# One strided tensor_reduce in place of three adds, in a kernel that subtracts the mean of every four rows

## The chip, the cores and the metric

One core of a Trainium2 chip. The metric is the device time of one execution in microseconds (us). Every time compared below is of runs in the fast state; the granted clock was 1.0 throughout. The two probe runs (p1, p2) ran once each, state unknown; only durations of single instructions are read from them. VectorE, the engine that does the sums, is called DVE in the profile. Data are worked on in SBUF, in 128 partitions (the 128 of the shapes in the profile); 16 DMA engines (the profile gives the queues' shares of 16) move them in (loads) and out (stores).

## The reference

```python
x_r = x.reshape(B, S // 4, 4, D)            # x: (8, 4096, 2112), float32
pooled = x_r.mean(axis=2)
return x - np.repeat(pooled, 4, axis=1)     # each row minus the mean of its group of four
```

## The kernel before

A group of four rows lies in one SBUF partition, 4 x 2112 = 8448 numbers one behind the other. 128 groups make a tile, and there are 64 tiles. For each: a load, three adds that make the sum `s`, one broadcast multiply-and-add that subtracts a quarter of it in place, and a store.

```python
STRIDE = 4
IO_BUFS = 6
# ... cut ...
    io_pool = ctx.enter_context(tc.tile_pool(name="io", bufs=IO_BUFS))
    sum_pool = ctx.enter_context(tc.tile_pool(name="sum", bufs=1))

    for g0 in range(0, G, P):
        gsz = min(P, G - g0)
        x_tile = io_pool.tile([P, W], mybir.dt.float32)
        nc.sync.dma_start(out=x_tile[:gsz], in_=xg[g0:g0 + gsz])

        rows = x_tile[:gsz].rearrange("p (f d) -> p f d", f=STRIDE)
        s = sum_pool.tile([P, D], mybir.dt.float32)
        nc.vector.tensor_add(out=s[:gsz], in0=rows[:, 0, :], in1=rows[:, 1, :])
        for f in range(2, STRIDE):
            nc.vector.tensor_add(out=s[:gsz], in0=s[:gsz], in1=rows[:, f, :])
        nc.vector.scalar_tensor_tensor(
            out=rows,
            in0=s[:gsz, None, :].to_broadcast([gsz, STRIDE, D]),
            scalar=-1.0 / STRIDE,
            in1=rows,
            op0=mybir.AluOpType.mult,
            op1=mybir.AluOpType.add,
        )
        nc.scalar.dma_start(out=og[g0:g0 + gsz], in_=x_tile[:gsz])
```

## Time and profile before

| | before |
|---|---|
| time, median | 1286.5 us |
| span in the profile | 1284.7 us |
| mean transfer rate over the span | 431 GB/s |
| VectorE busy | 1026.1 us (80%) |
| VectorE per tile: three adds, one subtract | 7.07 + 8.96 us |
| period of a tile in the middle | 19.95 us |

The rate is the row to start with: the 16 DMA engines are busy in practically every slice (the two queues take 50.0 and 49.9% of their time), so the kernel is bound by its transfers. The last three rows give the room that VectorE has in a tile; the prediction works it out and shows the lines behind the table.

### The profile page before, as it was taken

The page shows a single profiled execution, that of the slowest core. Times are in us where ns is not written, and L with a number is a line of the kernel's source. Part 1 is how long each engine was busy: PE and PEld are TensorE (multiplying, and loading weights), DVE is VectorE, ACT ScalarE, POOL GpSimd, SP SyncE. Part 2 cuts the span into 40 slices and gives each one's busy share as a digit, 9 for nine tenths or more (in the row PEclk, how much of TensorE's full clock was granted, in tenths as well). Part 3 has the DMA queues.
Part 4 walks back from the last instruction along what each step waited for, and adds up shares of the span by engine and source line. Part 5 has one row for each costly group of instructions (what it writes and reads, how often), then busy time and mean ns, then how long its engine had stood idle before and what let it go on. Part 6 is the DMA issues. An engine that isn't in the chain of part 4 may idle for free.

```text
span 1284.7 us, 674 instructions
## 1 busy us (share of the span) xinstructions
DVE 1026.1 (80%) x256; POOL 0.2 (0%) x4
## 2 busy tenths in 40 slices
DVE  5998778787787877878778787787887878778784
POOL 0000000000000000000000000000000000000000
DMA  9999999999999999999999999999999999999998
GB/s 404 421 438 438 433 425 437 438 427 432 437 437 426 435 437 431 429 437 437 431 428 438 437 431 429 437 436 432 428 438 436 430 430 437 437 426 433 438 431 380
DMA packets 18437, 553.70 MB, mean 431 GB/s; under 512 B 2048, under 2 KB 2048, under 8 KB 2048
## 3 DMA queue, kind: packets, MB, share of 16 engines
q1 hardware_dynamic: 9216, 276.83, 50.0%
q10 hardware_dynamic: 9216, 276.83, 49.9%
q14 instruction: 5, 0.04, 0.0%
HBM read 276.82 MB, written 276.82 MB: 431 GB/s over the span
## 4 chain that ended last, share of the span: by engine, by line
DVE 80%; another core or an unknown queue 17%; DMA 1%; issue 1%; DVEq 0%
DVE x_tile L46 45%; DVE s L45 24%; DVE s L43 12%; DMA x_tile<-in_x_dram 1%; DVEq L43 0%
## 5 line engine op out<-in xcount | busy, mean ns | idle before, releaser
L46 DVE SCALAR_TENSOR_TENSOR x_tile<-s,x_tile 128x8448 f32<-128x8448 f32 x64 | 573.3, 8958 | 2.2
L43 DVE TENSOR_TENSOR s<-x_tile 128x2112 f32<-128x2112 f32 x64 | 150.9, 2358 | 237.5 <-DMA x_tile<-in_x_dram 237.3
L45 DVE TENSOR_TENSOR s<-s,x_tile 128x2112 f32<-128x2112 f32 x128 | 301.8, 2358 | 4.4
L69 POOL MEMSET const-bfloat16-1.0<- 128x1 bf16 x1 | 0.1, 103 | 0.0
L69 POOL MEMSET const-uint8-127<- 128x1 uint8 x1 | 0.1, 102 | 0.0
L69 POOL MEMSET const-float32-0.0<- 128x1 f32 x1 | 0.1, 100 | 0.2 <-issue 0.2
L69 POOL MEMSET const-float32-1.0<- 128x1 f32 x1 | 0.1, 99 | 0.0
## 6 DMA issues: line engine op xcount, KB each, us to landing
x_tile<-in_x_dram SPq DMA_DIRECT2D x64, 4224.0 KB, 59.6
out_dram<-x_tile ACTq DMA_DIRECT2D x64, 4224.0 KB, 43.8
```

Of the source, the lines that this page charges most:

```text
L43: nc.vector.tensor_add(out=s[:gsz], in0=rows[:, 0, :], in1=rows[:, 1, :])
L45: nc.vector.tensor_add(out=s[:gsz], in0=s[:gsz], in1=rows[:, f, :])
L46: nc.vector.scalar_tensor_tensor(out=rows, in0=s[:gsz, None, :].to_broadcast([gsz, STRIDE, D]), scalar=-1.0 / STRIDE, in1=rows, op0=mybir. ...
L69: nc = _bacc.Bacc("TRN2", target_bir_lowering=False, num_devices=1)
```

## The change

Its intent: one instruction for the sum instead of three, with fewer fixed costs and no partial sums written and read back.

```diff
-        nc.vector.tensor_add(out=s[:gsz], in0=rows[:, 0, :], in1=rows[:, 1, :])
-        for f in range(2, STRIDE):
-            nc.vector.tensor_add(out=s[:gsz], in0=s[:gsz], in1=rows[:, f, :])
+        nc.vector.tensor_reduce(
+            out=s[:gsz],
+            in_=rows.rearrange("p f d -> p d f"),
+            op=mybir.AluOpType.add,
+            axis=mybir.AxisListType.X,
+        )
```

## The prediction

"The full rate" is that of line 46: 8958 ns for 8448 elements and 2358 for the adds' 2112 are 1.04 ns per element and 158 ns of fixed cost, and the 0.16 and 158 below are this cost. The forecast's sum came to 1286.5 + about 1.5 = 1288. The first rival's came to 1552.

> **What bounds the kernel now.** I read the page from the top: busy shares, then DMA in slices, then the queues, to see which resource has no slack; then the groups of instructions, for what one VectorE (DVE) tile costs; then two stretches of the trace, to see who waits for whom in the middle and what the end hangs on.
>
> ```profile
> span 1284.7 us, 674 instructions
> DVE 1026.1 (80%) x256; POOL 0.2 (0%) x4
> ...
> DMA  9999999999999999999999999999999999999998
> ...
> q1 hardware_dynamic: 9216, 276.83, 50.0%
> q10 hardware_dynamic: 9216, 276.83, 49.9%
> ...
> HBM read 276.82 MB, written 276.82 MB: 431 GB/s over the span
> ```
>
> The 16 DMA engines are at 90% or more in every slice but the last; one queue loads, the other stores, and together they take 99.9% of the engines' time. The bytes are already the least possible (x read once, the result written once). VectorE is busy 80% only. So the bound is DMA; VectorE counts only if it becomes slower than a tile's transfers. How far is that?
>
> ```profile
> L46 DVE SCALAR_TENSOR_TENSOR x_tile<-s,x_tile 128x8448 f32<-128x8448 f32 x64 | 573.3, 8958 | 2.2
> L43 DVE TENSOR_TENSOR s<-x_tile 128x2112 f32<-128x2112 f32 x64 | 150.9, 2358 | 237.5 <-DMA x_tile<-in_x_dram 237.3
> L45 DVE TENSOR_TENSOR s<-s,x_tile 128x2112 f32<-128x2112 f32 x128 | 301.8, 2358 | 4.4
> ```
>
> There are 64 tiles. Each has one add at line 43, two at line 45 (3 x 2.358 = 7.074 us) and one broadcast subtract at line 46 (8.958 us): 16.03 us busy. Nearly all of VectorE's idle time, 237.3 us, stands before the first add of a tile and is a wait for the load of x.
>
> ```profile
> 1194.25 2.36 DVE L43 TENSOR_TENSOR s<-x_tile 128x2112 f32<-128x2112 f32 x1 [3.83 <-DMA x_tile<-in_x_dram]
> ...
> 1214.20 2.36 DVE L43 TENSOR_TENSOR s<-x_tile 128x2112 f32<-128x2112 f32 x1 [3.81 <-DMA x_tile<-in_x_dram]
> ```
>
> A tile starts every 1214.20 - 1194.25 = 19.95 us, and VectorE sits idle 3.8 us of it. Between instructions lie about 0.03 us: early tiles, whose data lie ready, follow each other at 29.23 - 13.05 = 16.18 us, 0.14 more than the busy sum, for four instructions. So 3.8 us per tile is the room that the change may use up. The end, in five stretches:
>
> ```profile
> 1234.00:1254.00 20.00, 16.04 (x4) 0.00 (x0) 1.00 1.01 434
> 1254.00:1262.00 8.00, 7.78 (x4) 0.00 (x0) 1.00 0.95 410
> 1262.00:1270.00 8.00, 8.00 (x1) 0.00 (x0) 1.00 1.03 444
> 1270.00:1278.00 8.00, 0.26 (x1) 0.00 (x0) 1.00 1.01 435
> 1278.00:1285.00 7.00, 0.00 (x0) 0.00 (x0) 1.00 0.39 169
> ```
>
> The last load has landed at 1254, the last subtract ends at 1270.26 and the last store follows. From 1270 on 8 x 435 + 7 x 169 = 4.66 thousand KB move, where one store is 4.33 (4224 KB): when the last store is issued, only 0.33 MB of earlier stores is left, 0.8 us at 435 GB/s. In this tail VectorE is on the path almost in full.
>
> [...]
>
> **The change part by part.** Removed: 3 x 64 adds, 452.7 us of VectorE. Added: 64 reduces that read x_tile as (d, f), so successive reads lie 2112 x 4 = 8448 bytes apart and every fourth returns to the next column. Instruction order shows nothing else moves: loads and stores keep order and queues, the six x buffers and the single s stay, so there are still two dependent groups per tile, on one engine. Gaps fall from four to two, 0.07 us less.
>
> Cost at the full rate[...], as line 46 has it. That is 1.88 us more than the three adds, not less[...]. A tile takes 8.96 + 8.96 + 0.07 = 17.99 us. This is below 19.95, so it lies beside the transfers and the wait of 3.8 us shrinks to about 1.95. Buffers: a tile's load takes 59.6 us to land, its work 16, its store 43.8, and 119.4 is six periods of 19.95 (119.7): the loop is full because the DMA queues are, so 1.9 us more on VectorE just leaves 1.9 us less queueing. The start too: by the third store at 31 + 2 x 18 = 67 us there is work for at least 10 transfers of 10 us, so DMA never runs dry. The end: 1.88 us later less the 0.8 us of backlog used up, so +1.1 to +1.9. Sum: 1286.5 + about 1.5 = 1288.
>
> **The rivals.** First, VectorE becomes the bound because of the stride. The room is a reduce of 19.95 - 8.96 - 0.07 = 10.92 us, or (10.92 - 0.16)/8.448 = 1.27 ns per element. [...] with the first load (13.05 us before the first add), 13.7 for the last store without backlog, and 1.8 for the difference between timed run and span: 1552. At half rate (2.08 ns) 17.76 us and 1743[...]. For it: each successive element hops[...]. [...]
>
> Second, the gain that the change seems to intend: three instructions into one, fewer fixed costs. Two saved of 158 ns each are 20 us over 64 tiles, but VectorE isn't the bound[...]. Even an impossibly short reduce would save only part of the 16 us in the tail, at most 7 us or 0.5%. Faster by over 2% has no path.
>
> Third, the reduce at full rate, but 18 us too near to 19.95, so that jitter in loads starves the queues. The waits in the middle are even (3.71 to 3.85 us), and up to three tiles queue ahead; I give it next to nothing, 1290 to 1295 at most.
>
> **Range and chances.** Two outcomes, nothing much between: full rate and 1288, or a stride penalty. I lean to the full rate, 58 in 100[...]; I put 28 on penalties up to about 1.75 ns per element (1300 to 1560) and 13 on worse. The time is the first mode, put at 1289 to lean slightly to the rivals. The range must reach from the first mode through the second: 1284 to 1570, about 86%, the remainder above. Slower by 2% means 1312, a reduce beyond about 11 us, so nearly any penalty above 1.29 ns.
>
> **What would show it.** Right: one line of 64 TENSOR_REDUCE with a mean near 8957 ns, VectorE busy 64 x 17.92 = 1147 us (89%), the wait for loads cut from 237 to about 120 us, DMA still at 9 in every slice, the span longer by 1 to 2 us. Wrong: a reduce mean above 10.9 us; then the wait for loads vanishes after the first tile, VectorE stands near 98%, and the DMA digits fall to 8 or 7. If the reduce is slow but the time unchanged, the room was misread; if it is near 9 us and the time over 1295, the queue argument failed.

## The result, and the profile after

The changed kernel takes 1529.8 us (median of 5 runs, 1529.76 to 1530.04), the kernel before 1286.5 on the same chip. The ratio is 1.189, 95% interval 1.187 to 1.191: slower. Here and below, a ratio is the mean time of one kernel's fast runs over that of the other's of the same rounds, so it isn't quite the ratio of the medians quoted.

First the changed kernel's page: busy shares, the span in 40 slices (a digit is a busy share in tenths), the bytes moved.

```profile
span 1528.3 us, 546 instructions
...
DVE 1498.2 (98%) x128; POOL 0.2 (0%) x4
...
DVE  6999999999999999999999999999999999999996
...
DMA  9999899989899998998998989998989899889535
...
HBM read 276.82 MB, written 276.82 MB: 362 GB/s over the span
```

VectorE has gone from 80% to 98% and is busy 90% or more in every slice but the first and the last. The DMA digits, 9 in all slices but one before, drop to 8 in many slices and near the end to 3: the engines now wait for work. The same bytes move at 362 instead of 431 GB/s. The bound has changed hands. The groups of instructions of the changed kernel say which one did it, and its landing times what became of the queues:

```profile
L44 DVE TENSOR_REDUCE s<-x_tile 128x2112 f32<-128x8448 f32 x64 | 924.9, 14452 | 15.6 <-DMA x_tile<-in_x_dram 13.4
L50 DVE SCALAR_TENSOR_TENSOR x_tile<-s,x_tile 128x8448 f32<-128x8448 f32 x64 | 573.3, 8958 | 2.2
...
x_tile<-in_x_dram SPq DMA_DIRECT2D x64, 4224.0 KB, 21.2
out_dram<-x_tile ACTq DMA_DIRECT2D x64, 4224.0 KB, 22.6
```

The subtract is unchanged at 8958 ns. The reduce takes 14452 ns where the three adds took 3 x 2358 = 7074. The adds (2112 elements, 2358 ns) and the subtract (8448, 8958) lie on a line of 1.04 ns per element and 158 ns of fixed cost. Less that 158, the reduce takes 14294 / 8448 = 1.69 ns per element read. The wait for loads, 237.3 us before, is 13.4, the one before the first tile. A load now lands in 21.2 us (59.6 before) and a store in 22.6 (43.8): the queues are short, and a buffer spends its time with VectorE (an estimate from these medians: with six buffers, one comes round in six periods of 23.48, 140.9 us; its transfers take 43.8 of it, where they took 103.4 of 119.7 before). One tile in the timeline of the changed kernel:

```profile
1234.31 14.45 DVE L44 TENSOR_REDUCE s<-x_tile 128x2112 f32<-128x8448 f32 x1
...
1248.80 8.96 DVE L50 SCALAR_TENSOR_TENSOR x_tile<-s,x_tile 128x8448 f32<-128x8448 f32 x1
1257.79 14.45 DVE L44 TENSOR_REDUCE s<-x_tile 128x2112 f32<-128x8448 f32 x1
```

The period is 1257.79 - 1234.31 = 23.48 us, and the span adds up: 13.4 before the first reduce, 64 x 23.48 = 1502.7, and 12.3 from the end of the last subtract (1516.0) to the end, together 1528.4. The end of the changed kernel in three stretches (VectorE busy, then DMA share and GB/s last):

```profile
1504.00:1512.00 8.00, 7.97 (x2) 0.00 (x0) 1.00 0.00 0
1512.00:1520.00 8.00, 4.02 (x1) 0.00 (x0) 1.00 0.47 203
1520.00:1529.00 9.00, 0.00 (x0) 0.00 (x0) 1.00 0.70 300
```

While VectorE finishes the last tile, nothing moves at all; the last store then starts on idle engines.

### The profile page after: what moved, and what is told of

Same layout as the page of the kernel before. It is cut to its first block, busy times and chain, and to the rows that moved or that the text cites. A ratio compares the mean times of both kernels' runs of the same rounds, so it can differ in the third digit from the quotient of the medians.

```text
span 1528.3 us, 546 instructions
## 1 busy us (share of the span) xinstructions
DVE 1498.2 (98%) x128; POOL 0.2 (0%) x4
## 2 busy tenths in 40 slices
DMA packets 18436, 553.69 MB, mean 362 GB/s; under 512 B 2048, under 2 KB 2048, under 8 KB 2048
## 4 chain that ended last, share of the span: by engine, by line
DVE 98%; DMA 1%; issue 0%
DVE s L44 61%; DVE x_tile L50 38%; DMA x_tile<-in_x_dram 1%
## 5 line engine op out<-in xcount | busy, mean ns | idle before, releaser
L44 DVE TENSOR_REDUCE s<-x_tile 128x2112 f32<-128x8448 f32 x64 | 924.9, 14452 | 15.6 <-DMA x_tile<-in_x_dram 13.4
L50 DVE SCALAR_TENSOR_TENSOR x_tile<-s,x_tile 128x8448 f32<-128x8448 f32 x64 | 573.3, 8958 | 2.2
## 6 DMA issues: line engine op xcount, KB each, us to landing
x_tile<-in_x_dram SPq DMA_DIRECT2D x64, 4224.0 KB, 21.2
out_dram<-x_tile ACTq DMA_DIRECT2D x64, 4224.0 KB, 22.6
```

The costliest lines, as they stand in the source:

```text
L44: nc.vector.tensor_reduce(out=s[:gsz], in_=rows.rearrange("p f d -> p d f"), op=mybir.AluOpType.add, axis=mybir.AxisListType.X,)
L50: nc.vector.scalar_tensor_tensor(out=rows, in0=s[:gsz, None, :].to_broadcast([gsz, STRIDE, D]), scalar=-1.0 / STRIDE, in1=rows, op0=mybir. ...
```

## The experiments

Three questions. Is it the stride, or the reduce as such, that makes 14.45 us? Does the length of VectorE's tile explain the time? And what would a reduce at the full rate have given? The diffs are shortened; `...` stands for what is left out.

**e1_adjacent: the same reduce over neighbours.** The result is wrong (each group of four is four columns of one row).

```diff
-            in_=rows.rearrange("p f d -> p d f"),
+            in_=x_tile[:gsz].rearrange("p (d f) -> p d f", f=STRIDE),
```

> Same reduce of groups of four, but over four neighbouring elements instead of over the four rows (the result is wrong on purpose). Theory 1 (the stride is what costs): the reduce takes about 8.96 us,[...] VectorE is busy 89%, and the time is 1288 us, as the first branch of the prediction had it. Theory 2 (a reduce in groups of four is slow whatever it reads): 14.45 us and about 1530 us as in the changed kernel. If the reduce takes 9 us and the time is still over 1295, my reading of the room beside the transfers is wrong.

(The subtract over as many elements took 8958 ns in the kernel before.)

Measured: 1318.6 us, ratio 1.025 (1.024 to 1.027). From this run's page:

```profile
L44 DVE TENSOR_REDUCE s<-x_tile 128x2112 f32<-128x8448 f32 x64 | 573.0, 8953 | 154.5 <-DMA x_tile<-in_x_dram 154.2
...
HBM read 276.82 MB, written 276.82 MB: 420 GB/s over the span
```

The same instruction, the same shapes, the same number of groups: 8953 ns instead of 14452. So the addresses cost the 5.5 us, and the reduce as such does not. But the time is not the 1288 that went with that branch, though VectorE waits 154 us for loads, so it isn't the bound. The transfers themselves are slower, 420 in place of 431 GB/s. That part of my reading was wrong; e6 to e8 go after it.

**p1_patterns: what a hop costs.** The changed kernel with four x buffers, and on the first four tiles 18 extra instructions into a scratch tile, each on its own line. For instance:

```diff
+            nc.vector.tensor_reduce(out=scr[:, 0:W // 2].rearrange("p (b d) -> p b d", d=4224),
+                in_=x_tile[:, 0:W].rearrange("p (b f d) -> p b d f", f=2, d=4224), op=..., axis=...)
```

> The changed kernel with four x buffers; the first four tiles also run 18 probe instructions into a scratch tile, each on a line of its own (time of the whole is of no interest; results stay right). Theory 1[...]: groups of four at hop 1 take 8.96 us; every other hop (2, 4, 16, 24, 64, 1056, 2112 words) is slower, 14 us or more[...]; pairs of neighbours and then a hop take 8.96. Theory 2: all groups of four take 14.45, groups of two 19.9 (5.49 us too much for 2112 groups is 2.6 ns a group), groups of eight 11.7. Theory 3 (a single read stream is free to alternate between two regions, and it is four regions or the distance that costs): groups of two at 4096 and 4224 words take 8.53 and 8.96 us, while groups of four and eight are slow; hop 2048 instead of 2112 tells whether the distance matters. A copy that reads the same hops, and an add with one hopping source, say whether other instructions pay as well[...].

The result was right; the run took 2350.9 us, which means nothing here. "Group" is how many elements are summed, "hop" the distance in 4-byte words from one to the next. Eight of its groups of instructions:

```profile
L49 DVE TENSOR_REDUCE scr<-x_tile 128x2112 f32<-128x8448 f32 x4 | 60.4, 15109 | 0.1
L64 DVE TENSOR_TENSOR scr<-x_tile 128x8448 f32<-128x8448 f32 x4 | 59.0, 14754 | 0.1
...
L54 DVE TENSOR_REDUCE scr<-x_tile 128x2112 f32<-128x8448 f32 x4 | 57.8, 14453 | 0.1
...
L57 DVE TENSOR_REDUCE scr<-x_tile 128x4224 f32<-128x8448 f32 x4 | 36.2, 9041 | 0.1
...
L63 DVE TENSOR_TENSOR scr<-x_tile 128x8448 f32<-128x8448 f32 x4 | 35.8, 8958 | 0.1
L60 DVE TENSOR_REDUCE scr<-x_tile 128x1056 f32<-128x8448 f32 x4 | 35.8, 8953 | 0.1
...
L48 DVE TENSOR_REDUCE scr<-x_tile 128x2112 f32<-128x8448 f32 x4 | 35.8, 8944 | 0.0
...
L62 DVE COPY scr<-x_tile 128x8448 f32<-128x8448 f32 x4 | 29.7, 7415 | 0.1
```

L54 is the reduce of the change. L49 is a group of four at a hop of only 4 words: as slow, even slower. Hops of 16, 24, 64 and 1056 words lie between 14274 and 14523, and 2048 words (8 KiB) at 14017 for its 8192 elements, the same rate (1.69 ns per element). So the distance hardly matters. L57 is a group of **two**, 4224 words apart: 9041, nearly free; at 4096 words (16 KiB) 8773 for 8192 elements. Groups of eight at 1056 words: 14341. L60 reads two neighbours before each hop: free (8953). A hop of 1 is free (8948), and L48, a hop of 2 words, is free too, against theory 1. L64 is an add one of whose sources goes over the four rows: 14754 against 8958 for the contiguous add in L63, and the copy pays as well (L62, 7415 against 4559 contiguous). Theory 2 falls. Theory 3 fits the large hops: two regions in turn are free, four are not.

**p2_patterns: where the edge lies.** Fourteen more probes built the same way.

> A second set of 14 probes on the first four tiles (time of the whole of no interest). In the first set groups of four over four regions took 14.45 us at hops of 64, 1056 and 2112 words, over two regions 9.04, groups of four at hop 2 words 8.94, pairs of neighbours then a hop 8.95. Theory P[...]: groups of two are free at any hop (about 9.0 us at 2, 4, 16, 24); groups of three at hop 16 and 2816 are slow, over 11 us; groups of four at hop 3 slow; groups of eight and sixteen at hop 2 free[...], groups of eight at hop 4 slow. Theory Q (it is three or more regions at great distance): groups of eight at hop 4 free, of three at 2816 slow. Theory R (only groups of four and more pay): groups of three free. If the free two-region pattern belongs to a single read stream only, the add with one source over two regions takes 14.75 us as it did over four;[...] 8.96. The copy over two regions, 4.56 if free, 7.4 if not.

The result was right (2069.5 us, again without meaning). Five of its groups:

```profile
L55 DVE TENSOR_REDUCE scr<-x_tile 128x1056 f32<-128x8448 f32 x4 | 60.4, 15108 | 0.1
...
L51 DVE TENSOR_REDUCE scr<-x_tile 128x2816 f32<-128x8448 f32 x4 | 39.3, 9831 | 0.1
...
L58 DVE TENSOR_TENSOR scr<-x_tile 128x8448 f32<-128x8448 f32 x4 | 36.5, 9125 | 0.1
...
L53 DVE TENSOR_REDUCE scr<-x_tile 128x2112 f32<-128x8448 f32 x4 | 35.8, 8953 | 0.1
L56 DVE TENSOR_REDUCE scr<-x_tile 128x528 f32<-128x8448 f32 x4 | 35.8, 8953 | 0.1
```

Groups of two took 8946, 9077, 9024 and 9129 ns at hops of 2, 4, 16 and 24 words: within 2% of the 8953 of neighbours (L60) at each of them. Groups of three (L51, hop 2816; 9636 at hop 16) pay a tenth at most, where theory P wanted over 11 us. Groups of four pay in full, except at hops of 2 (8944 in p1) and 3 words (L53, 8953); the latter P also called slow. At a hop of 2110 words, no multiple of four, they take 14441 for 8440 elements, so it isn't a matter of even spacing in steps of four words. Groups of 8 and 16 at a hop of 2 words are free (8954, and L56), groups of 8 at 4 words are the slowest (L55). The free two-region pattern isn't confined to a single read stream: the add with one source over two regions takes 9125 (L58), and the copy 4639. So P is wrong, and so are Q (groups of eight at 4 words are near each other and slow) and R only nearly right. What stands is what was measured at these hops: reading 8448 elements in turn, one at a time, from two places is free within 2% (8946 to 9129 ns), from three nearly (9636 and 9831), from four or eight at hops of 4 words and more it costs 60 to 70% (14274 to 15109). Why the edge lies there was not settled.

**e2_half_of_tiles and e3_three_quarters: does VectorE's length explain the time?** Right results both.

```diff
+        if (g0 // P) % 2 == 0:      # e3: (g0 // P) % 4 != 3
+            nc.vector.tensor_reduce(...)   # strided, as in the change
+        else:
+            nc.vector.tensor_add(...)      # the three adds
```

> The strided reduce on even tiles, three adds on odd ones; right result. Buffers average the two: VectorE needs 32 x (23.48 + 16.17) = 1269 us, a mean of 19.83 per tile and just under the 19.95 of the transfers; with 13.4 before and some 13 after, 1295 to 1310 us. If each slow tile cost its own excess over the transfers (no averaging): 32 x (23.48 + 19.95) + 27 = 1417 us.

> The strided reduce on three tiles of four, adds on the fourth; right result. VectorE's mean tile is (3 x 23.48 + 16.18)/4 = 21.65 us, above the 19.95 of the transfers, so VectorE bounds: 64 x 21.65 + 13.4 + 12.3 + 1.8 = 1413 us, transfers at some 390 GB/s. If each slow tile cost its own excess over 19.95 with no averaging: 64 x (3 x 23.48 + 19.95)/4 + 27 = 1473 us.

Measured: 1296.1 us for half (ratio 1.007, 1.006 to 1.009), 1412.9 for three quarters (1.098, 1.097 to 1.100), each where the averaging account put it (1295 to 1310, and 1413) and at least 60 us away from the other. The six buffers average slow and fast tiles, so what counts is the mean VectorE time of a tile against the 19.95 us of its transfers. With half of the tiles strided, both are at their limit at once, as its page shows:

```profile
DVE 1262.2 (98%) x192; POOL 0.2 (0%) x4
...
HBM read 276.82 MB, written 276.82 MB: 428 GB/s over the span
```

**e4_one_add: is there anything to gain from a cheaper sum?** Two of the three adds are left out. Its output is wrong, which doesn't matter for the time.

```diff
         nc.vector.tensor_add(out=s[:gsz], in0=rows[:, 0, :], in1=rows[:, 1, :])
-        for f in range(2, STRIDE):
-            nc.vector.tensor_add(out=s[:gsz], in0=s[:gsz], in1=rows[:, f, :])
```

> The kernel before with two of its three adds left out (wrong on purpose): VectorE has 11.4 us a tile instead of 16.2. Theory: transfers bound, so only the tail can gain, and there 4.7 us at most and rather 1 to 3, since earlier stores fill the engines: 1283 to 1286 us, the wait for loads up from 237 to some 540 us. If VectorE's time were on the path, it would be up to 306 us shorter.

Measured: 1285.9 us, ratio 0.9995 (0.998 to 1.001). VectorE's busy time fell by 302 us to 724, the wait for loads rose to 543.5, and the time stayed.

```profile
L43 DVE TENSOR_TENSOR s<-x_tile 128x2112 f32<-128x2112 f32 x64 | 150.9, 2358 | 543.5 <-DMA x_tile<-in_x_dram 543.5
```

So a sum at a third of its cost gives nothing here, and the change's intent had nothing to win. The tail wasn't shortened either, because the last tile began later: its first add at 1258.59 us instead of 1254.12, its subtract done at 1269.94 instead of 1270.26.

**e6, e7, e8: why did e1 take 1318 and not 1288?** The kernel before with a dead partial add ahead of the three (N = 1543, 700 and 2112 columns), which lengthens VectorE's tile to 17.98, 17.10 and 18.57 us. Right results. These ran on another chip than e1, each beside the kernel before.

```diff
+        nc.vector.tensor_add(out=s[:gsz, :N], in0=rows[:, 0, :N], in1=rows[:, 1, :N])  # filler
         nc.vector.tensor_add(out=s[:gsz], in0=rows[:, 0, :], in1=rows[:, 1, :])
```

> The kernel before, with an extra add of the first 1543 columns ahead of the three adds (dead work, right result): 1.765 us more, so VectorE has 17.98 us a tile, as with the reduce of neighbours, but not one reduce. That run took 1318.6 us in place of 1288, its transfers at 420 instead of 431 GB/s. Theory A (it is the moment at which stores are issued relative to the loads that costs, so only the length of VectorE's tile counts): again about 1318 us and 420 GB/s. Theory B (the reduce reads SBUF in a way that disturbs the transfers): 1288 us and 431 GB/s.

> The same with 700 columns: 17.10 us a tile. Theory A: if it is a matter of how near VectorE comes to the period of 19.95, between the kernel before and the 18.0 run, 1290 to 1310; theory B: 1287.5 us.

> The same with all 2112 columns, a fourth full add: 18.57 us a tile. Theory A by nearness: above 1318. Theory B: 1289. If it is lower than the 18.0 run, it is not nearness but a coincidence of moments at one length (half of the tiles with the reduce, 19.83 in the mean, kept 433 GB/s).

Measured: 1320.7 us (ratio 1.026, 1.025 to 1.028) at 17.98; 1308.1 to 1317.3 in the three fast runs at 17.10 (1.022, 1.020 to 1.025; the mean of the three over the kernel before is 1.0205); and 1286.6 (1.001, 0.999 to 1.003) at 18.57, the longest, where one run of four took 1292.5. A fourth run at 17.10, 1411.1, counts as slow and is left out; its clock was 1.0 and it left no trace, so what slowed it isn't known. The transfer rates by slice, first of the 17.98 run, then of the 17.10 run, then of the 18.57 run:

```profile
GB/s 411 415 437 427 425 428 430 422 425 426 419 429 422 427 425 424 426 418 423 434 420 427 420 424 425 416 423 421 416 426 420 425 416 425 422 414 424 419 412 334
```

```profile
GB/s 412 409 409 402 420 414 422 417 427 430 431 429 433 434 433 434 437 430 433 435 433 434 435 431 433 434 433 436 434 431 434 434 432 437 434 431 435 433 358 313
```

```profile
GB/s 404 421 438 438 435 424 437 437 433 427 437 437 430 430 437 437 427 432 438 433 428 435 437 433 427 437 435 436 425 438 436 435 426 438 435 431 430 438 435 377
```

Plain adds with the tile length of e1 lose about as much (2.6%, e1 2.5%), so theory B falls: it doesn't take the reduce to disturb the transfers. Nor is it nearness to 19.95, since 18.57 is nearer and costs next to nothing. The timing of VectorE's tile is what is left of the causes tried, by elimination, and it works in a narrow range (ratios 1.022 and 1.026 at 17.10 and 17.98 us, 1.001 at 18.57).

The engines are not idle meanwhile. The queues of the 17.98 run, loads first:

```profile
q1 hardware_dynamic: 9216, 276.83, 50.6%
q10 hardware_dynamic: 9216, 276.83, 48.9%
```

Together 99.5% of 1316.8 us, against 99.9% of 1284.7 before, for the same packets: most of the loss is in packets that take longer, above all those of loads (666 us an engine, before 642). In the packet records, 900 of the 8192 large load packets took over 1.35 us, where the median is 1.25; before it was 48. In the 17.10 run the longer packets are mostly those of stores, early on.

In the landing events of the traces (one from each of the 16 engines for a transfer), the spread between first and last grows from 1 to 19 us over the 17.98 run, and stays under 3 us in the kernel before and in the 18.57 run. So the engines drift apart. In the 17.10 run the spread passes 17 us in the first fifth and then stays at some 19 to 26 us, while the rate is back at 433: the slow slices there are the first nine and the last two. Being apart costs nothing in the middle, then; growing apart goes with the loss, and so does the end. What makes packets longer at these tile lengths was not settled.

**e10_quarter: the same mean, other moments.** The strided reduce on every fourth tile, a mean of 18.0 us, right result.

```diff
+        if (g0 // P) % 4 == 3:      # the rest as in e2
```

> The strided reduce on one tile of four: mean tile 18.0 us, the same as in the two runs that lost 2.5% (1318 and 1320), but made of tiles of 16.18 and 23.48. If the mean length is what slows the transfers, about 1318 us at 420 GB/s; if it is the moment at which each store follows, which now shifts from tile to tile, 1287 to 1300 us.

Measured: 1291.7 us (ratio 1.004, 1.003 to 1.006), with 433 GB/s from 120 to 1240 us. So the mean length is not what slows the transfers. Of the regular tiles, those of 17.10 and 17.98 us did, those of 16.18 and 18.57 did not. The 5 us that remain over the kernel before lie at the end, where the last tile is a strided one. The last subtract in the kernel before, then here:

```profile
1261.30 8.96 DVE L46 SCALAR_TENSOR_TENSOR x_tile<-s,x_tile 128x8448 f32<-128x8448 f32 x1
...
1268.71 8.96 DVE L55 SCALAR_TENSOR_TENSOR x_tile<-s,x_tile 128x8448 f32<-128x8448 f32 x1
```

Both last tiles begin at the same moment (1254.12 and 1254.23), the subtract ends 7.4 us later, and the span is 5.2 us longer: from 1270 to 1278 us only 51 GB/s move here, before 435.

**e11_split_tail: a version that might beat both.** In the last tile alone the subtract and the store are cut into four, one for each row. Right result.

```diff
+            for f in range(STRIDE):      # last tile only
+                nc.vector.scalar_tensor_tensor(out=rows[:, f, :], in0=s[:gsz], scalar=-1.0 / STRIDE,
+                    in1=rows[:, f, :], op0=mult, op1=add)
+                nc.scalar.dma_start(out=og[g0:g0 + gsz, f * D:(f + 1) * D], in_=rows[:, f, :])
```

> The kernel before, with the subtract and the store of the last tile alone cut into four, one for each row of a group; right result. The first quarter of the last store is issued about 6.6 us earlier, when some 3 MB of earlier stores are still under way, so the engines need not idle, and only the last quarter (1.08 MB, 2.5 us) follows the last subtract: 3 to 4 us less than before, 1282.5 to 1283.5. If the tail is bound by the bytes anyway, under 1 us.

Measured: 1286.8 us, ratio 1.000 (0.999 to 1.002): a miss. The first of the four stores did start 6.4 us earlier (1263.9 instead of 1270.3), but from 1270 to 1278 us the engines moved 408 GB/s where the kernel before had 435, and the end fell at the same moment. Why was not settled. It doesn't say what an earlier finish of VectorE would give, since the last subtract ended at 1270.7 here and at 1269.9 in e4, hardly another moment than the 1270.3 before. No version here beat the kernel before.

## Why the prediction was right or wrong

The range, 1284 to 1570, held the 1529.8 us because it was made to reach through the first rival. The outcome that the point stood for, 1289, did not come, and the point was 241 us low: what came was the first rival, to which together with worse strides the prediction gave 41 in 100.

- **Bound and room: right.** Transfers bound the kernel before, and 19.95 us is where VectorE takes over. e2 and e3 measured 1296.1 and 1412.9, where that number put them (1295 to 1310, and 1413).
- **The step that failed: "I lean to the full rate, 58 in 100", and with it the cost of 8957 ns; it measured 14452.** The ground for the lean was the author's estimate. p1 and p2 show that the number of regions matters: two 9.04 us, three 9.8, four 14.45; and one source or two makes no difference (add over two regions 9.1, over four 14.75). It isn't the number of elements either: e1's reduce reads and writes as many and takes 8953 ns.
- **The rival's working: right in that the stride made VectorE the bound, 22 us high in size.** Its sum was 1552; its time per element, an estimate that rested on no trace of this case, is cut. Measured were 1.69 ns per element and 14.45 us. The last store took 12.3 instead of 13.7. The signs it named were seen: wait for loads gone after the first tile, VectorE at 98%, DMA digits falling.
- **The buffers: right in one place and wrong in another.** "1.9 us more on VectorE just leaves 1.9 us less queueing" failed in e1 (1318.6 instead of 1288) and in e6 with plain adds, and held at 18.57 us. So the reduce at the full rate that could be tried, e1's, was 2.5% slower, a branch that I gave next to nothing; the prediction had no term for it, and the profile of before did not show it.
- **No path to faster: supported** by e4, where 302 us less work on VectorE gave 0.7 us, within the noise.
- **The end: mis-sized.** "1.88 us later less the 0.8 us of backlog used up" takes a longer tile to delay the last subtract by as much. In e8 every tile is 2.4 us longer, yet the last subtract ended at 1270.11 (before 1270.26), because the last tile began 2.5 us earlier, at 1251.58; in e4, with tiles 4.8 us shorter, it began 4.5 us later. In e10, where the last tile did end late, 7.4 us of delay made the span 5.2 us longer: VectorE is on the path there, but 2.2 us were absorbed and not 0.8.

## What to carry to other kernels

Count what an instruction reads, and the number of places it reads from in turn: the three adds need 7.07 us, one reduce over the same 8448 elements 8.95 if they are neighbours, and 14.45 if they come in turn from four rows. An engine that idles has only the room that its waits show; here 3.8 us per tile, and a change that adds 7.4 makes it the bound. And a VectorE change that fits in the room can still move the time by 2 or 3% (2.5% in e1, 2.6% in e6), here through longer packets whose cause stays open: measure it, don't only add it up.
